# A hybrid layer in fp32r: low parts of 14 weight chunks by an accumulating DMA, the second input chunk in halves, score masks in pairs

## The chip, the cores and the metric

The kernel runs on one core of a Trainium2 chip. Its engines are TensorE (PE, with its weight loads PEld), VectorE (DVE), ScalarE (ACT), GpSimd (POOL) and SyncE (SP), which issues most DMAs. The metric is the device time of one execution in microseconds.

## What is computed

One layer: eight heads of block-sparse attention and four heads of an mLSTM share one input projection; their joined output goes through w_out, and a squared-ReLU MLP follows.

```python
D_MODEL = 1024; SEQ = 512; ATT_HEADS = 8; ATT_HEAD_DIM = 64; MLSTM_HEADS = 4; D_FF = 4096

def hybrid_layer(x, positions, ...):
    hdn = rms_norm(x, g_mix_pre)
    proj = hdn @ w_in
    aq, ak, av, mq, mk, mv, mo, mi, mf = jnp.split(proj, ...)
    q_a = partial_rope(to_heads(aq, ATT_HEADS), positions)
    k_a = partial_rope(to_heads(ak, ATT_HEADS), positions)
    att = moba_attention(q_a, k_a, v_a)
    ...
    hm = mlstm_chunkwise(q_m, k_m, v_m, ig, lf)
    ...
    mixed = jnp.concatenate([att, hm], axis=-1).astype(x.dtype)
    x = x + rms_norm(mixed @ w_out, g_mix_post)
    u = rms_norm(x, g_mlp_pre) @ w_up
    u = jnp.square(jax.nn.relu(u))
    return x + rms_norm(u @ w_down, g_mlp_post)
```

All inputs are float32. With 512 tokens and blocks of 256, attention is plain causal attention in effect: each of the four 128-query tiles of a head sees the keys up to its own end, and a triangular mask is added on the diagonal 128x128 block.

## The kernel before

Every float32 product is made of three fp32r matmuls: an operand is split into a high part (rounded to fp32r) and a low part (the rest), and high x high, high x low and low x high are summed in PSUM.

The weights come in chunks, numbered in the order of use: 0 to 3 for the mLSTM's q and k (mqk), 4 to 7 for the gates and part of v (gv, 392 columns a half), 8 to 11 and 16 to 19 for the attention's q and k (qk), 12 to 15 (vv) and 20 to 23 (av) for v, 24 to 27 for the output gate, 28 to 35 for w_out, from 36 on for the MLP. Each chunk is loaded by SP into one of three `raw` buffers (line 171). `split_to` (lines 180 to 200) then makes its parts in one of three `ws` buffers: ScalarE copies `raw` into `ws[:,0]`, which rounds it (line 197), and VectorE subtracts that from `raw` into `ws[:,1]` (line 198). For the odd chunks 5 to 35 GpSimd does the subtraction. `chunk(i)` asks for the split of chunk i+2 and the load of chunk i+4 when PE's program reaches chunk i. Within a slab PE takes, for each weight part, x-high by weight-high, then x-high by weight-low, then x-low by weight-high (in mqk: weight-high by x-high, weight-high by x-low, weight-low by x-high), so the low part is wanted a step or two after the high part.

At the start, x comes transposed in four chunks (`xr0` to `xr3`), with weight chunks 0 to 2 between them (lines 263 to 271). The first x chunk and weight chunk 0 are loaded in halves. `split_x` makes high and low parts of x (lines 252 and 253). After mqk, PE transposes a row of normalisation factors (`rstd_rows`, line 318 on; tiles rc, pb, rb), and gv follows.

PE's order is written by hand: `Flow` interleaves the side work (mLSTM and attention heads) with the weight slabs by planned times. The other engines are ordered by priorities, where a chunk's split ranks ahead (offset `BOOST`). In `att_head` each head handles its four score tiles in two pairs. For a tile it issues two fp32r matmuls (query by key-high, key-low), a third bf16 one that adds the mask (`identb` x `maskb`, line 672), then on VectorE the row maximum (line 674), on ScalarE the exponential (line 676), and on VectorE the reciprocal and the scaling by it (lines 677 and 678).

Of the kernel before, what the change touches and what calls it, by code (L numbers as in the profile page):

```python
# [15 lines left out]
F32 = mybir.dt.float32  # L16
# [4 lines left out]
OP = mybir.AluOpType  # L21
# [3 lines left out]
P = 128  # L25
S = 512
# [81 lines left out]
def kernel(  # L108
# [17 lines left out]
    nc = tc.nc  # L126
    f = lambda ap: ap.bitcast(F32)
# [3 lines left out]
    ring = ctx.enter_context(tc.tile_pool(name="ring", bufs=3))  # L131
# [3 lines left out]
    psa = ctx.enter_context(tc.tile_pool(name="psa", bufs=4, space=PSUM))  # L135
# [3 lines left out]
    specs = []  # L139
# [24 lines left out]
    raws, splits = {}, {}  # L164
    state = {"res": None, "load": 0, "split": 0}
# [8 lines left out]
    def load_to(i):  # L174
        while state["load"] <= min(i, len(specs) - 1):
            k = state["load"]
            raws[k] = load_raw(specs[k][0], specs[k][1], f"raw{k}")
            state["load"] += 1

    def split_to(i):  # L180
        while state["split"] <= min(i, len(specs) - 1):
            k = state["split"]
            if specs[k][2] == "res" and state["res"] is None:
                return
            load_to(k)
            _, n, where = specs[k]
            if where == "ring":
                ws = ring.tile([P, 2, 1024], F32R, tag="ws", name=f"ws{k}", bufs=3)
            else:
                ws = state["res"].tile([P, 2, 1024], F32R, tag="u", name=f"ws{k}")  # L190
            raw = raws.pop(k)
            parts = 2 if k == 0 else 1
            lo = nc.gpsimd if 3 < k < n_wo and k % 2 else nc.vector
            with tc.high_priority(offset=BOOST):
                for a in range(parts):
                    sl = slice(a * n // parts, (a + 1) * n // parts)
                    nc.scalar.copy(ws[:, 0, sl], raw[:, sl])  # L197
                    lo.tensor_tensor(ws[:, 1, sl], raw[:, sl], f(ws[:, 0, sl]), op=OP.subtract)  # L198
            splits[k] = ws
            state["split"] += 1  # L200

    def chunk(i):

        split_to(i + 2)
        load_to(i + 4)
        return splits[i]

    def mm(o, lh, rh, first, last, go_on=False):
        nc.tensor.matmul(o, lh, rh, start=first, stop=last, skip_group_check=go_on)  # L209
        flow.pe(max(o.shape[-1], 256) / 2.4 + 2.5)  # L210
# [6 lines left out]
    def tr(o, i, idn):  # L217
        nc.tensor.transpose(o, i, idn)  # L218
        flow.pe(109.0)
# [36 lines left out]
    xv = x_t.rearrange("p k n -> p (k n)")  # L256
    def spare(tag, name):
        return wk.tile([P, 1280], F32, tag=tag, name=name, **({"bufs": 3} if tag == "w5" else {}))

    xrs = [spare(("w5", "w5", "w5", "h5")[c], f"xr{c}") for c in range(4)]  # L260
    raws[0] = ring.tile([P, 1024], F32, tag="raw", name="raw0", bufs=3)
    state["load"] = 1
    for a in range(2):
        sl = slice(a * S, (a + 1) * S)
        nc.sync.dma_start(xrs[0][:, sl], xv[:, sl])
        nc.sync.dma_start(raws[0][:, sl], specs[0][0][:, sl])
    for c in range(1, 4):
        nc.sync.dma_start(xrs[c][:, 0:1024], xv[:, c * 1024:(c + 1) * 1024])
        if c < 3:
            load_to(c)  # L270
# [6 lines left out]
    for c in range(4):  # L277
        split_x(c, xrs[c])
        if c < 3:
            split_to(c)  # L280
# [140 lines left out]
    for c, ci in enumerate(slab_chunks["mqk"]):  # L421
        ws = chunk(ci)
# [9 lines left out]
    identb = one.tile([P, P], BF16, name="identb")  # L432
    maskb = one.tile([P, P], BF16, name="maskb")
# [216 lines left out]
    def att_head(g, h):  # L650
        e = h % 2
        half = slice(64 * e, 64 * e + 64)
        pr = 2 * g + h // 2
        hid = 4 * g + h
        prev = [f"st{g}a" if h < 2 else f"st{g}b"] + ([f"h{hid - 2}"] if hid >= 2 else [])
        for ii in ((0, 1), (2, 3)):
            yield dict(cond=prev if ii[0] == 0 else None, banks=2, hold=DLY["sh"])
            if ii[0] == 0:
                qs, ks, kls = stacks[g]
                if e == 0:  # L660
                    mix[pr] = kts.tile([P, 2, S], F32R, tag="kt", name=f"mix{pr}")
                    m32s[pr] = wk.tile([P, S], F32, tag="t32", name=f"m32_{pr}")
                pp = wk.tile([P, 1280], F32, tag="w5", name=f"pp{g}{h}", bufs=3)
                mxs = small.tile([P, NT], F32, tag="mxs", name="mxs", bufs=3)
                rs = small.tile([P, NT], F32, tag="rs", name="rs", bufs=3)
            for i in ii:
                n = (i + 1) * P
                sp = psa.tile([P, S], F32, tag="at", name=f"as{g}{h}{i}")
                iq = slice(i * P, (i + 1) * P)
                mm(sp[:, 0:n], qs[h][:, iq], ks[h][:, 0:n], True, False)  # L670
                mm(sp[:, 0:n], qs[h][:, iq], kls[h][:, 0:n], False, False)
                nc.tensor.matmul(sp[:, i * P:n], identb, maskb, start=False, stop=True)
                flow.pe(56)
                nc.vector.tensor_reduce(mxs[:, i:i + 1], sp[:, 0:n], axis=AX.X, op=OP.max, negate=True)  # L674
                po = pp[:, POFF[i]:POFF[i] + n]
                nc.scalar.activation(po, sp[:, 0:n], AF.Exp, bias=mxs[:, i:i + 1], accum_out=rs[:, i:i + 1])  # L676
                nc.vector.reciprocal(rs[:, i:i + 1], rs[:, i:i + 1])
                nc.vector.tensor_scalar(po, po, rs[:, i:i + 1], None, op0=OP.mult)
        ph = wk.tile([P, 1280], F32R, tag="h5", name=f"ph{g}{h}")
        pl = wk.tile([P, 1280], F32R, tag="l5", name=f"pl{g}{h}")  # L680
        for jj in ((0, 1), (2, 3)):
            yield dict(delay=DLY["pt"] if jj[0] == 0 else 0, banks=2, hold=DLY["pth"])
            for j in jj:
                n = S - j * P
                pt = psa.tile([P, S], F32, tag="at", name=f"pt{g}{h}{j}")
                for i in range(j, NT):
                    tr(pt[:, (i - j) * P:(i - j + 1) * P], pp[:, POFF[i] + j * P:POFF[i] + (j + 1) * P], ident)
                c = slice(OFF[j], OFF[j] + n)
                nc.scalar.copy(ph[:, c], pt[:, 0:n])
                nc.vector.tensor_tensor(pl[:, c], pt[:, 0:n], f(ph[:, c]), op=OP.subtract)  # L690
        yield dict(delay=DLY["ao"], banks=1, hold=1500, cond=f"av{g}")
        o = psa.tile([P, S], F32, tag="at", name=f"ao{g}{h}")
        for j in range(NT):
            c = slice(OFF[j], OFF[j] + S - j * P)
            mm(o[:, j * P:], av[g][j][:, h], ph[:, c], j == 0, False)
            mm(o[:, j * P:], av[g][j][:, h], pl[:, c], False, j == NT - 1)
        m32 = m32s[pr]
        nc.scalar.copy(m32[half], o[64:128])
        nc.vector.tensor_tensor(m32[half], o[0:64], m32[half], op=OP.add)
        if e == 1:  # L700
            nc.scalar.copy(mix[pr][:, 0], m32)
            nc.vector.tensor_tensor(mix[pr][:, 1], m32, f(mix[pr][:, 0]), op=OP.subtract)
        flow.flags.add(f"h{hid}")
# [5 lines left out]
    for g in range(2):  # L709
        flow.add(att_group(g))  # L710
        for h in range(4):
            flow.add(att_head(g, h))
# [42 lines left out]
    for i, c in enumerate(WO_ORDER):  # L755
        flow.until(need[c])
        ws = chunk(wo_chunks[0][i])
# [188 lines left out]
    at, bt = {}, {}  # L946
# [49 lines left out]
    for g in range(3):  # L996
        new_group(g + 1)
        for m in range(8):
            n = 7 * g + m
# [31 lines left out]
    for c in range(4):  # L1031
        ws = chunk(dn_chunks[0, c])
# [13 lines left out]
    for t in range(NT):  # L1046
        cuts = [(0, S)] if t < NT - 1 else [(0, 256), (256, 512)]
        yg = ygs[t]
        for a, b in cuts:
            pd = (psa if a == 0 else psm).tile([P, S], F32, tag="at" if a == 0 else "mm", name=f"dl{t}{a}")[:, a:b]  # L1050
            for m in range(8):
                c, kc = m // 2, slice((m % 2) * S + a, (m % 2) * S + b)
# [81 lines left out]
```

## Time and profile before

| | |
|---|---|
| median of 3 runs | 593.75 us (592.96 to 594.2) |
| profiled execution | 595.46 us, span 593.7 us, mean granted clock 0.995 |
| PE busy | 578.5 us (97%), 2895 matmuls |
| DVE busy | 429.4 us (72%) |
| ACT busy | 286.4 us (48%) |
| POOL busy | 72.6 us (12%) |
| DMA | 60.79 MB, mean 102 GB/s |
| chain that ended last | PE 87%, DVE 8%, ACT 2%, DMA 1% |

Busy time is the time in which an engine has an instruction in work; matmuls are pipelined, so a PE that is busy may still step more slowly than it can. The chain follows the last instruction back through whatever released each step. The granted clock is TensorE's, as a share of full speed.

### The profile page before, as it was taken

The page shows a single profiled execution, that of the slowest core. Times are in us where ns is not written, and L with a number is a line of the kernel's source. Part 1 is how long each engine was busy: PE and PEld are TensorE (multiplying, and loading weights), DVE is VectorE, ACT ScalarE, POOL GpSimd, SP SyncE. Part 2 cuts the span into 40 slices and gives each one's busy share as a digit, 9 for nine tenths or more (in the row PEclk, how much of TensorE's full clock was granted, in tenths as well). Part 3 has the DMA queues.
Part 4 walks back from the last instruction along what each step waited for, and adds up shares of the span by engine and source line. Part 5 has one row for each costly group of instructions (what it writes and reads, how often), then busy time and mean ns, then how long its engine had stood idle before and what let it go on. Part 6 is the DMA issues. An engine that isn't in the chain of part 4 may idle for free.

```text
span 593.7 us, 7757 instructions
## 1 busy us (share of the span) xinstructions
PE 578.5 (97%) x2895; PEld 488.6 (82%) x2895; DVE 429.4 (72%) x790; ACT 286.4 (48%) x505; POOL 72.6 (12%) x78
## 2 busy tenths in 40 slices
PE   8999999899999999999999999999999999999995
PEld 4898898688978888898888888888888888888884
DVE  5897868687996845865778685988667986856346
ACT  5664556467756654475344344344443443444211
POOL 0133341225311040000000000000000000000132
PEclk9999999899999999999999999999999999999999
DMA  7633121102311266007611363121543114013002
GB/s 281 258 135 115 63 71 55 35 20 72 107 71 36 73 230 231 0 1 257 257 54 36 110 218 132 36 68 40 198 156 106 36 36 142 35 36 129 14 35 108
DMA packets 18470, 60.79 MB, mean 102 GB/s; under 512 B 2432, under 2 KB 2432, under 8 KB 18432
## 3 DMA queue, kind: packets, MB, share of 16 engines
q1 hardware_dynamic: 18288, 60.28, 29.3%
q8 instruction: 23, 0.38, 0.3%
q14 instruction: 15, 0.12, 0.1%
q10 hardware_dynamic: 144, 0.01, 0.0%
HBM read 58.19 MB, written 2.10 MB: 102 GB/s over the span
## 4 chain that ended last, share of the span: by engine, by line
PE 87%; DVE 8%; ACT 2%; DMA 1%; issue 1%; SPq 0%; DVEq 0%; ACTq 0%
PE up L209 29%; PE pX L209 11%; PE qk L209 7%; PE pY L209 5%; PE mo L209 4%; PE dl L209 4%; PE ya L209 4%; PE dn L209 4%; PE gv L209 3%; PE pZ L209 3%; PE mqk L209 3%; PE vv L209 2%; PE yb L209 2%; PE ao L209 1%; PE as L209 1%; PE pt L218 1%
## 5 line engine op out<-in xcount | busy, mean ns | idle before, releaser
L209 PE MATMUL up<-hT,ws 128*128 128x512 f32 (+1 forms) x840 | 180.0, 372 | 0.4 <-DVE hT L811 0.4
L209 PEld LDWEIGHTS up<-hT,ws 128*128 128x128 f32 x840 | 148.3, 188 | 27.8 <-DVE hT L811 0.6
L197 ACT CAST ws<-raw 128x1024 fp32r<-128x1024 f32 (+3 forms) x77 | 76.3, 996 | 127.6 <-PE up L209 83.7
L198 DVE TENSOR_TENSOR ws<-raw,ws 128x1024 fp32r<-128x1024 f32 (+3 forms) x61 | 73.0, 1198 | 62.2 <-ACT ws L197 61.7
L904 ACT CAST w<-b 128x1024 fp32r<-128x1024 f32 x42 | 44.3, 1055 | 61.5 <-PE pX L209 27.2
L905 DVE TENSOR_TENSOR w<-b,w 128x1024 fp32r<-128x1024 f32 x42 | 51.4, 1223 | 25.9 <-ACT w L904 25.9
L209 PE MATMUL pX<-w,a 128*128 128x512 f32 x288 | 67.2, 389 | 0.0
L209 PEld LDWEIGHTS pX<-w,a 128*128 128x128 f32 x288 | 54.1, 188 | 11.2
L198 POOL TENSOR_TENSOR ws<-raw,ws 128x1024 fp32r<-128x1024 f32 (+3 forms) x16 | 36.5, 2284 | 115.2 <-ACT ws L197 79.9
L209 PE MATMUL qk<-ws,xT 128*128 128x512 f32 x192 | 49.2, 406 | 0.0
L1043 POOL TENSOR_TENSOR yg<-y,gp 128x512 f32<-128x512 f32 x4 | 5.2, 1299 | 337.4 <-DVE y L1038 337.2
L209 PEld LDWEIGHTS qk<-ws,xT 128*128 128x128 f32 x192 | 36.0, 193 | 7.0
L209 PE MATMUL pY<-w,a 128*128 128x512 f32 x144 | 33.6, 389 | 0.0
L209 PEld LDWEIGHTS pY<-w,a 128*128 128x128 f32 x144 | 27.0, 188 | 5.6
L876 DVE TENSOR_TENSOR b<-b,b 128x1024 f32<-128x1024 f32 x24 | 29.1, 1218 | 1.4 <-DMA b<-in_w_down_dram 1.3
L209 PE MATMUL mo<-ws,xT 128*128 128x512 f32 x96 | 25.9, 407 | 0.0
L209 PE MATMUL mqk<-xT,ws 128*128 128x512 f32 x96 | 23.5, 397 | 1.4 <-ACT ws L197 0.9
L209 PEld LDWEIGHTS mqk<-xT,ws 128*128 128x128 f32 x96 | 17.6, 188 | 7.4 <-ACT ws L197 2.2
L209 PE MATMUL yb<-ws,mix 128*128 128x512 f32 x96 | 23.1, 394 | 0.0
L209 PE MATMUL ya<-ws,mix 128*128 128x512 f32 x96 | 22.9, 394 | 0.0
L676 ACT ACTIVATE pp<-as,mxs 128x128 f32<-128x128 f32 (+3 forms) x32 | 16.8, 526 | 11.0 <-DVE mxs L674 10.9
L904 ACT CAST a<-u 128x1024 fp32r<-128x1024 f32 x17 | 17.8, 1050 | 8.8 <-DVE u L846 4.9
(283 smaller groups left out, 930.9 us busy)
## 6 DMA issues: line engine op xcount, KB each, us to landing
raw<-in_w_up_dram SPq DMA_DIRECT2D x32, 512.0 KB, 3.3
b<-in_w_down_dram SPq DMA_DIRECT2D x24, 512.0 KB, 4.4
raw<-in_w_in_dram SPq DMA_DIRECT2D x15, 512.0 KB, 3.3
raw<-in_w_out_dram SPq DMA_DIRECT2D x8, 512.0 KB, 3.3
raw<-in_w_down_dram SPq DMA_DIRECT2D x8, 512.0 KB, 3.2
xs<-in_x_dram SPq DMA_DIRECT2D x4, 512.0 KB, 8.7
x<-in_x_dram SPq DMA_DIRECT2D x4, 512.0 KB, 6.6
out_dram<-yg SPq DMA_DIRECT2D x8, 256.0 KB, 2.0
```

The source lines that it names most:

```text
L197: nc.scalar.copy(ws[:, 0, sl], raw[:, sl])
L198: lo.tensor_tensor(ws[:, 1, sl], raw[:, sl], f(ws[:, 0, sl]), op=OP.subtract)
L209: nc.tensor.matmul(o, lh, rh, start=first, stop=last, skip_group_check=go_on)
L218: nc.tensor.transpose(o, i, idn)
L676: nc.scalar.activation(po, sp[:, 0:n], AF.Exp, bias=mxs[:, i:i + 1], accum_out=rs[:, i:i + 1])
L876: nc.vector.tensor_tensor(o, a, b, op=op)
L904: nc.scalar.copy(o[:, 0], src)
L905: nc.vector.tensor_tensor(o[:, 1], src, f(o[:, 0]), op=OP.subtract)
L1043: nc.gpsimd.tensor_tensor(ygs[t][:, A], y[t][:, A], gp2[:, A], op=OP.mult)
```

## The change

Three edits. First, for the odd chunks from 5 to 31 (14 of the 16 that GpSimd split), ScalarE makes the low part's start: it writes the negative of `raw`, rounded, to `ws[:,1]`, and a DMA issued by GpSimd reads the chunk from DRAM once more and adds it there. Chunks 33 and 35 stay with GpSimd's subtraction. Second, the second x chunk and weight chunk 1 are loaded in halves, and chunk 1 is split in halves. Third, the scores of both tiles of a pair come first, then both masks in a row, then the work of VectorE and ScalarE on each.

```diff
-            parts = 2 if k == 0 else 1
+            parts = 2 if k < 2 else 1
...
                     nc.scalar.copy(ws[:, 0, sl], raw[:, sl])
-                    lo.tensor_tensor(ws[:, 1, sl], raw[:, sl], f(ws[:, 0, sl]), op=OP.subtract)
+                    if 3 < k < 32 and k % 2:
+
+                        nc.scalar.mul(ws[:, 1, sl], raw[:, sl], -1.0)
+                        nc.gpsimd.dma_start(ws[:, 1, sl], specs[k][0][:, sl], accum_op=OP.add)
+                    else:
+                        lo.tensor_tensor(ws[:, 1, sl], raw[:, sl], f(ws[:, 0, sl]), op=OP.subtract)
...
-    for c in range(1, 4):
+    raws[1] = ring.tile([P, 1024], F32, tag="raw", name="raw1", bufs=3)
+    state["load"] = 2
+    for a in range(2):
+        sl = slice(a * S, (a + 1) * S)
+        nc.sync.dma_start(xrs[1][:, sl], xv[:, 1024 + a * S:1024 + (a + 1) * S])
+        nc.sync.dma_start(raws[1][:, sl], specs[1][0][:, sl])
+    for c in range(2, 4):
...
+            sps = {}
             for i in ii:
                 n = (i + 1) * P
-                sp = psa.tile([P, S], F32, tag="at", name=f"as{g}{h}{i}")
+                sp = sps[i] = psa.tile([P, S], F32, tag="at", name=f"as{g}{h}{i}")
                 iq = slice(i * P, (i + 1) * P)
                 mm(sp[:, 0:n], qs[h][:, iq], ks[h][:, 0:n], True, False)
                 mm(sp[:, 0:n], qs[h][:, iq], kls[h][:, 0:n], False, False)
-                nc.tensor.matmul(sp[:, i * P:n], identb, maskb, start=False, stop=True)
+            for i in ii:
+                nc.tensor.matmul(sps[i][:, i * P:(i + 1) * P], identb, maskb, start=False, stop=True)
                 flow.pe(56)
+            for i in ii:
+                n = (i + 1) * P
+                sp = sps[i]
                 nc.vector.tensor_reduce(mxs[:, i:i + 1], sp[:, 0:n], axis=AX.X, op=OP.max, negate=True)
```

On GpSimd, at the gv slab, the two subtractions for chunks 5 and 7 (`ws5`, `ws7`) stood among the memsets that clear halves of the mLSTM's key tiles (`m2kl`, `m3kl`). Before:

```order
L198 TENSOR_TENSOR ws5_285<-raw5_230,ws5_285 128x784
L410 MEMSET m2kl0_344 64x512
L198 TENSOR_TENSOR ws7_412<-raw7_288,ws7_412 128x784
L410 MEMSET m2kl1_350 64x512
L410 MEMSET m3kl0_358 64x512
L410 MEMSET m3kl1_364 64x512
```

Now:

```order
L201 DMA ws5_289<-in_w_in_dram 128x784
L201 DMA ws7_417<-in_w_in_dram 128x784
L421 MEMSET m2kl0_349 64x512
L421 MEMSET m2kl1_355 64x512
L421 MEMSET m3kl0_363 64x512
L421 MEMSET m3kl1_369 64x512
```

The two transfers stand in a row, and all four memsets behind both.

On ScalarE, at the same place, between the casts of chunks 4 to 7 and the first parts of the mLSTM's queries (`m0q`, `m1q`). Before:

```order
L197 CAST ws4_256<-raw4_201 128x784
L197 CAST ws5_285<-raw5_230 128x784
L197 CAST ws6_383<-raw6_259 128x784
L398 ACTIVATE m0q0_327<-t32_0_325 64x512
L398 ACTIVATE m0q1_330<-t32_0_325 64x512
L398 ACTIVATE m1q0_335<-t32_1_333 64x512
L398 ACTIVATE m1q1_338<-t32_1_333 64x512
L197 CAST ws7_412<-raw7_288 128x784
```

Now:

```order
L197 CAST ws4_260<-raw4_205 128x784
L197 CAST ws5_289<-raw5_234 128x784
L200 ACTIVATE ws5_289<-raw5_234 128x784
L197 CAST ws6_388<-raw6_263 128x784
L409 ACTIVATE m0q0_332<-t32_0_330 64x512
L409 ACTIVATE m0q1_335<-t32_0_330 64x512
L197 CAST ws7_417<-raw7_293 128x784
L200 ACTIVATE ws7_417<-raw7_293 128x784
```

Line 200 is the multiplication by -1; it follows its chunk's cast, and chunk 7's two passes now stand ahead of the two `m1q` parts.

On PE, the second pair of score tiles of one head (`as`), up to the next head group's transposes (`tp`). Before:

```order
L209 MATMUL as_1719<-a03k_1134,a01q_1091 128x384
L209 MATMUL as_1719<-a03kl_1135,a01q_1091 128x384
L672 LDWEIGHTS identb
L672 MATMUL as_1719<-maskb,identb 128x128
L209 MATMUL as_1727<-a03k_1134,a01q_1091 128x512
L209 MATMUL as_1727<-a03kl_1135,a01q_1091 128x512
L672 LDWEIGHTS identb
L672 MATMUL as_1727<-maskb,identb 128x128
L218 MATMUL tp_1737<-cs,qk_1508 128x128
```

Now:

```order
L214 MATMUL as_1733<-a03k_1145,a01q_1101 128x384
L214 MATMUL as_1733<-a03kl_1146,a01q_1101 128x384
L214 MATMUL as_1736<-a03k_1145,a01q_1101 128x512
L214 MATMUL as_1736<-a03kl_1146,a01q_1101 128x512
L685 LDWEIGHTS identb
L685 MATMUL as_1733<-maskb,identb 128x128
L685 LDWEIGHTS identb
L685 MATMUL as_1736<-maskb,identb 128x128
L223 MATMUL tp_1751<-cs,qk_1521 128x128
```

The first tile's mask has moved behind the second tile's two steps.

## Rows read from the trace of the kernel before

**Rows 1.** The page: busy time, share of the span and instructions of each engine, and the chain that ended last, by engine.

```profile
PE 578.5 (97%) x2895; PEld 488.6 (82%) x2895; DVE 429.4 (72%) x790; ACT 286.4 (48%) x505; POOL 72.6 (12%) x78
PE 87%; DVE 8%; ACT 2%; DMA 1%; issue 1%; SPq 0%; DVEq 0%; ACTq 0%
```

**Rows 2.** Busy time by stage: the stretch and its length in us, then the busy time and instructions of PE, PEld, DVE, ACT and POOL, the granted clock, the DMA engines' share and GB/s.

```profile
5.09:13.51 8.42, 7.31 (x26) 4.55 (x26) 4.85 (x8) 4.77 (x7) 0.00 (x0) 1.00 0.95 352
...
29.90:47.20 17.30, 17.30 (x100) 17.30 (x99) 15.10 (x25) 10.71 (x18) 7.53 (x7) 1.00 0.42 144
...
74.00:109.00 35.00, 31.42 (x194) 29.53 (x192) 28.09 (x70) 20.96 (x49) 9.63 (x13) 1.00 0.20 61
```

**Rows 3.** Timeline of PE at the start: start us, length us, what ran, and in brackets the idle time before it and what ended that.

```profile
8.64 3.28 PE L209 MATMUL mqk<-xT,ws 128*128 128x512 f32 x12 [0.22 <-ACT ws L197]
12.26 0.73 PE L209 MATMUL mqk<-xT,ws 128*128 128x512 f32 x2 [0.33 <-ACT ws L197]
13.51 16.21 PE L209 MATMUL mqk<-xT,ws 128*128 128x512 f32 x70 [0.52 <-DVE ws L198]
```

**Rows 4.** The chain, in order of time, at the end of the mqk slab and through gv: start us, length us, what.

```profile
29.72 0.44 PE pb L218 x4
30.16 17.08 PE gv L209 x96
```

**Rows 5.** Timeline of ScalarE and VectorE around the second x chunk and weight chunk 1.

```profile
9.86 1.34 ACT L252 ACTIVATE xT<-xr,gcol 128x512 fp32r<-128x512 f32 x2 [1.27 <-DMA xr<-in_x_t_dram]
...
11.15 1.05 ACT L197 CAST ws<-raw 128x1024 fp32r<-128x1024 f32 x1
12.23 1.22 DVE L198 TENSOR_TENSOR ws<-raw,ws 128x1024 fp32r<-128x1024 f32 x1 [0.20 <-ACT ws L197]
```

**Rows 6.** Timeline of ScalarE, VectorE and GpSimd around the start of gv. In order: the casts of chunks 4 and 5, the copy for the transposes, GpSimd's low part of chunk 5, VectorE's of chunk 4, the copy after the transposes, VectorE's low part of chunk 6, the cast of chunk 7, GpSimd's low part of chunk 9.

```profile
26.30 1.58 ACT L197 CAST ws<-raw 128x784 fp32r<-128x784 f32 x2
...
27.91 0.42 DVE L323 COPY rc<-rstd 128x512 f32<-128x512 f32 x1
27.96 2.99 POOL L198 TENSOR_TENSOR ws<-raw,ws 128x784 fp32r<-128x784 f32 x1 [9.54 <-ACT ws L197]
28.24 0.97 DVE L198 TENSOR_TENSOR ws<-raw,ws 128x784 fp32r<-128x784 f32 x1
...
30.20 0.69 DVE L326 COPY rb<-pb 128x512 f32<-128x512 f32 x1 [0.99 <-PE pb L218]
30.80 0.98 DVE L198 TENSOR_TENSOR ws<-raw,ws 128x784 fp32r<-128x784 f32 x1
...
35.04 0.85 ACT L197 CAST ws<-raw 128x784 fp32r<-128x784 f32 x1
...
44.24 2.40 POOL L198 TENSOR_TENSOR ws<-raw,ws 128x1024 fp32r<-128x1024 f32 x1 [4.55 <-issue]
```

**Rows 7.** DMA issues, with the KB of each and the median us from issue to landing. The first row is of the loads issued from 16 to 21 us, the other two are of 28.9 to 31.9 us, where the first is a queue's row: packets, MB and the share of 16 engines.

```profile
raw<-in_w_in_dram SPq DMA_DIRECT2D x3, 392.0 KB, 8.5
...
q1 hardware_dynamic: 144, 0.40, 38.7%
...
raw<-in_w_in_dram SPq DMA_DIRECT2D x1, 392.0 KB, 2.8
```

**Rows 8.** Groups of instructions by form over the whole span: busy us, mean ns of one, and the idle time before them with what ended it. ScalarE's casts of weight chunks, then GpSimd's low parts.

```profile
L197 ACT CAST ws<-raw 128x1024 fp32r<-128x1024 f32 x63 | 65.9, 1052 | 113.9 <-PE up L209 83.7 <-issue 17.5 <-DMA raw<-in_w_out_dram 5.3
...
L197 ACT CAST ws<-raw 128x512 fp32r<-128x512 f32 x6 | 3.7, 617 | 3.8 <-DMA raw<-in_w_in_dram 3.2 <-POOL qk L622 0.6
...
L197 ACT CAST ws<-raw 128x784 fp32r<-128x784 f32 x4 | 3.3, 842 | 1.9 <-issue 1.9
...
L198 POOL TENSOR_TENSOR ws<-raw,ws 128x1024 fp32r<-128x1024 f32 x10 | 25.2, 2522 | 84.3 <-ACT ws L197 49.0 <-issue 23.5 <-DVE pp L678 11.8
```

**Rows 9.** Timeline of PE at one pair of score tiles: the first tile's second step, its mask, and the second tile's two steps. Lengths overlap, since matmuls are pipelined; the starts tell the pace.

```profile
124.48 0.33 PE L209 MATMUL as<-a02kl,a00q 128*128 128x384 f32 x1
124.66 0.23 PE L672 MATMUL as<-maskb,identb 128*128 128x128 bf16 x1
124.70 0.47 PE L209 MATMUL as<-a02k,a00q 128*128 128x512 f32 x1
125.01 0.40 PE L209 MATMUL as<-a02kl,a00q 128*128 128x512 f32 x1
```

**Rows 10.** Timeline rows of GpSimd, VectorE and PE: GpSimd's low part of chunk 23 and a scaling of scores beside it, PE's wait at 156.40 and its first step with chunk 23, and a scaling of the same form at another place.

```profile
147.68 1.28 POOL L198 TENSOR_TENSOR ws<-raw,ws 128x512 fp32r<-128x512 f32 x1 [4.27 <-ACT ws L197]
147.75 1.29 DVE L678 TENSOR_SCALAR pp<-pp,rs 128x128 f32<-128x128 f32 x1
...
156.40 0.30 PE L218 MATMUL pt<-cs,pp 128*128 128x128 f32 x1 [0.82 <-DVE a12kl L412]
156.46 0.72 PE L209 MATMUL av<-ws,xT 128*128 128x256 f32 x4
...
170.22 0.28 DVE L678 TENSOR_SCALAR pp<-pp,rs 128x128 f32<-128x128 f32 x1
```

**Rows 11.** PE's wait in the attention part and the slab's steps behind it, from the timeline, and one microsecond of the table by stretches (columns as in rows 2).

```profile
108.69 0.33 PE L209 MATMUL sp<-m1q,m3k 128*128 128x128 f32 x1 [2.57 <-DVE dd L569]
...
108.97 4.50 PE L209 MATMUL qk<-ws,xT 128*128 128x512 f32 x12
...
110.00:111.00 1.00, 1.00 (x4) 0.81 (x3) 0.90 (x2) 1.00 (x2) 0.00 (x0) 0.50 0.00 0
```

## What was predicted before the change was run

> **What bounds the kernel now.** I read the page's busy line and the chain that ended last first [rows 1]. TensorE is busy 578.5 of 593.7 us and carries 87% of the chain; VectorE comes next with 8%. So a saving counts only where PE waits or takes a step longer than it must. The table by stage [rows 2] says where that can be. The chunks from 32 on, which the change leaves alone, fill more than the second half of the span. In what comes before, PE stands idle in few places: 1.1 us of the 8.42 around the second chunk at the start and 3.6 us of the 35 from 74 to 109. PE also steps at half clock for some 3 us after 109. The timelines, read at these places, show what is late. At the start [rows 3] PE waits 0.33 us for ScalarE's cast of the second chunk and 0.52 us for VectorE's low part of it, and runs without a gap from 13.51 to 29.72, where the chain goes on to the transposes and the gv slab [rows 4]. Behind both waits stands a transfer: the second x chunk has landed only when ScalarE takes it up at 9.86, the chunk's weights at 11.15 [rows 5], with the DMA engines 95% busy [rows 2]. In the attention part PE waits 2.57 us at 108.69 for VectorE, which is busy 28.09 of the 35 us before [rows 2], and behind that wait the clock is granted at 0.50, the lower of its two levels (1.2 GHz) [rows 11].
>
> **The start by halves: -0.8.** Two loads of 512 KB become four of half the size, in the order x, weights, x, weights, and the two passes of the second chunk's split become four. The bytes are the same, so the last half lands where the whole did, near 11.1; the first half of x and of the weights land before that, I reckon by 9.9, where the whole x chunk landed. A cast of 512 columns is 0.62 us [rows 8], so the first half's high part is there by about 10.5 to 11.2 and its low part some 0.7 us later (half of the 1.22 us that the whole took, and a little [rows 5]). PE ends the first chunk at 11.92 [rows 3] and then needs only that first half; the second half is wanted twelve steps of 0.23 us later (70 of them take 16.21 us [rows 3]), at 14.7, long after 12.5. Both waits go, 0.33 + 0.52 = 0.85. What is late next is the end of the slab: it comes at 28.9 instead of 29.72. The four transposes there need VectorE's copy that ends at 28.33, and the next slab needs VectorE's low part of chunk 4, which ends at 29.21 [rows 6]; the slab's second step would now stand at 29.3. That is tight, so I take -0.8, with -0.3 (that low part or the copies slip) and -0.9 as ends.
>
> **The masks in a row: -0.8.** The rows at 124.48 [rows 9] show the price of one: the score step of 384 columns before it takes 0.18 us, as a gv step of 392 does [rows 4], the mask itself holds PE for 0.04 (124.66 to 124.70), but the fp32r step behind it takes 0.31 (124.70 to 125.01), where one of 512 columns otherwise takes 0.23. A mask thus makes the next step 0.08 us longer. With two in a row, one of each pair has a mask behind it, not an fp32r step. The trace has no mask behind a mask. If it takes the 0.04 us of a mask, 16 pairs give 16 x 0.08 = -1.3; if the cost merely moves to it, nothing. I take -0.05 a pair, -0.8. The first tile's maximum can start only after the second tile's two steps, some 0.55 us later. VectorE has other work for that time, and in the attention part the waits of PE that I price are for other products (108.69 and 156.40).
>
> **GpSimd's subtractions gone: -0.4.** Fourteen of its sixteen low parts, 2.5 us each for 1024 columns [rows 8], leave the engine. It was 12% busy, so its own time is worth nothing. But VectorE stood still beside one: a 128x128 multiplication that takes 0.28 us elsewhere took 1.29 beside GpSimd's 1.28 at 147.7 [rows 10]. Work of VectorE alone leads from there to PE's wait of 0.82 us at 156.40. Without those 1.01 us the wait could go whole, unless other work then moves in front; half of it is -0.4, the ends are 0 and -0.8.
>
> **Fourteen more passes on ScalarE: +0.3.** The multiplication by -1 reads and writes what the cast does; at its rows [rows 8] that is 8 x 1.052 + 4 x 0.842 (768 and 784 columns) + 2 x 0.617 = 13.0 us. ScalarE is 48% busy, which covers most of it. Where it isn't covered is 74 to 109 us, three such passes: ScalarE's casts and copies there feed the VectorE that PE waits for. A pass of 0.84 that delays that chain fully costs 0.8 each and may lengthen the stretch at half clock. A third of one is +0.3; the ends are +1.5 (two in full) and -1.0, since VectorE loses GpSimd's company there too.
>
> **Fourteen accumulating transfers: +0.7.** Each reads the chunk from HBM again and adds it to the negated high part, 6.2 MB in all; the DMA engines' share is 0.42 and 0.20 in two of these stages [rows 2], so bandwidth is there. What counts is when each lands. For chunk 5 ScalarE's two casts end at 27.88 [rows 6], its negation at 28.72, so GpSimd issues at about 28.8. Before, GpSimd had this low part at 30.95, and the first step of chunk 5 stood at 30.0 + 24 x 0.178 = 34.3 (the gv slab: 96 steps in 17.08 [rows 4]); with the earlier start it is 33.5, and the second step, the first to read the low part, 33.7. That leaves 4.9 us. The trace has no accumulating and no GpSimd-issued transfer. A plain one of this size took 2.8 us with free queues and 8.5 in the crowd at the start [rows 7]; these are my bounds. Reading its target as well as its source, it should be nearer to two of the quiet ones: 5.6, so 34.4, and PE waits 0.7. The ends are 0 (up to 4.9) and +3.6 (8.5). The other chunks have more. Chunk 7 is negated by 36.7 (its cast ends at 35.89 [rows 6]) and wanted at 30.0 + 72 x 0.178 + 0.2 = 43.0, 6.3 us; chunk 9 by 45.2 (GpSimd began at 44.24 [rows 6] as the cast ended) and wanted one slab end and 24 steps on, 47.24 (30.16 + 17.08) + 24 x 0.23 + 0.2 = 53.0, 7.8 us; chunk 23, cast by 147.7 as GpSimd began, by 148.3 and wanted behind its first step at 156.46 [rows 10], 156.6, 8.3 us. GpSimd's queue now holds four memsets behind the transfer of chunk 7, where one stood ahead of it and three behind; they start when ScalarE has negated chunk 7, near 36.7, earlier than the three behind GpSimd's subtraction of chunk 7 could, which began only as the cast ended.
>
> "DMA: Bandwidth & Descriptors" of the Trainium skill, in "Anatomy of one DMA", fits a GpSimd-issued transfer as about 2.0 us plus its bytes at 436 GB/s, an estimate of 2.9 us for 392 KB. That is the quiet row's 2.8; it has nothing on the added read. By it alone this term would be 0 and the sum 592.0.
>
> **The sum.** -0.8 - 0.8 - 0.4 + 0.3 + 0.7 = -1.0 us. The profiled execution took 595.46 with a span of 593.7; it would become 594.5 and 592.7. It lies 1.7 above the median of the timed runs, 593.75, to which I apply the same difference: **592.75**.
>
> **The rivals.**
> 1. *The stretch before 109 is relieved.* VectorE, free of GpSimd, reaches the product for which PE waits 2.57 us [rows 11] earlier, and PE doesn't fall to half clock: twelve steps at 108.97 took 4.50, 1.7 more than 12 x 0.23. Half of the wait and half of that loss are 1.3 + 0.9 = 2.2 us below the sum: 590.55. For it: VectorE nearly never pauses there. Against: I saw its stretching only beside GpSimd at 147.7, not there.
> 2. *The accumulating transfers land late* (slower than before). If one takes 9 us, chunk 5 is late by 4.1 instead of 0.7, and with PE later chunks 7 and 9 are then covered; chunk 23 adds 0.6. Net 3.4 + 0.6 = +4.0: 596.75. It comes out slower than before from a first transfer of 6.6 us (1.0 more late), and beyond what can be told from 7.8. For it: the same size took 8.5 here in a crowd. Against: at 28.8 the queues are nearly empty (38.7% busy from 28.9 to 31.9 [rows 7]).
> 3. *GpSimd can't issue beside VectorE.* In [rows 10] the two engines shut each other out. If an issue needs a pause of VectorE, and chunk 5's misses the one before the copy at 30.20, it goes out at about 31.8, when VectorE's next low part has ended [rows 6], and lands at 37.4: late by 3.7, a total near 595.75. For it: VectorE is busy 15.10 of the 17.30 us after 29.90 [rows 2]. Against: it does pause, 0.99 us before 30.20, and most of its work there are other forms than that of [rows 10].
> 4. *ScalarE's passes delay the stretch before 109* by one to two whole passes of 0.84 in place of a third of one, and the half clock lasts as much longer, for up to 0.8: 593.3 to 594.9.
>
> "SBUF - State Buffer" of the Trainium skill, in "SBUF: two separate sides", has rival 3 as a rule: transfers issued by GpSimd have their descriptors written by it, and it is locked out while VectorE holds the port that they share. The row at 147.7 agrees on the lock between the two engines' instructions; no row here shows an issue.
>
> **How the numbers follow.** The forecast, 592.0 to 594.0, has 0.47; rival 1 has 0.17, rival 2 0.13, rival 3 0.08, rival 4 0.15. About 0.2% of the time, 1.2 us, is what a measurement of this kernel can tell from no change, so faster means below 592.55 and slower above 594.95. Faster holds rival 1 and somewhat less than half of the forecast, 0.38; slower holds rivals 2 and 3 and a little of 4, 0.23; the rest, 0.39, is no change that can be told. The range leaves out the far ends of rivals 1 and 2: 590.4 to 597.0.
>
> **What would show it.** Start: no wait of PE between 11.9 and 28.9 and the gv slab beginning 0.8 us earlier; wrong, if a wait for VectorE's low part of chunk 1 or 4 appears. Masks: the step behind the second mask 0.31, the second mask itself within 0.1 us of the first. Transfers: on GpSimd's queue, the median from issue to landing for 392 KB and 512 KB (5.6 and 7 us by my estimate), and a PE wait for a DMA at the second step of chunk 5 of 0.7 us, none elsewhere. GpSimd: no VectorE multiplication of 1.29 us at 147. ScalarE: the wait at 108.69 as long as now, and the half clock too. The forecast is wrong most likely through the transfers, if PE waits for one later than chunk 5, or through the stretch before 109.

## The result and the profile after

The kernel became slower. Ten runs of the changed kernel have a median of 598.11 us (595.51 to 601.34), ten of the kernel before 594.33 (592.96 to 596.05); the ratio is 1.0053, with a 95% interval of 1.0035 to 1.0071, some +3.2 us (the two medians lie 3.8 apart). The prediction was 592.75 in a range of 590.4 to 597.0, with 0.23 for slower: the sign was wrong, and the time lies beyond the range.

The profiled execution is the fastest of the ten, with a span of 593.7 us, the same as that of the profile before; the other nine have spans of 594.4 to 599.6. So I read in this trace what the change does where nothing more is lost, and in a second one, of 599.1, what is added in a longer execution.

The page of the changed kernel, busy time and chain, against [rows 1]:

```profile
PE 576.9 (97%) x2895; PEld 488.2 (82%) x2895; DVE 424.3 (71%) x791; ACT 296.7 (50%) x520; POOL 52.9 (9%) x78
PE 85%; DVE 9%; ACT 2%; DMA 2%; issue 1%; DVEq 0%; SPq 0%; ACTq 0%
```

ScalarE is busy 10.3 us more: the 14 passes add up to 13.1 (13.0 were reckoned), part of it in overlap with other instructions. GpSimd is busy 20 less. The chain now has 2% of DMA.

Its table by stage, columns as in [rows 2]:

```profile
5.09:13.51 8.42, 8.30 (x36) 6.50 (x36) 5.26 (x9) 4.98 (x9) 0.00 (x0) 1.00 0.96 342
...
29.90:47.20 17.30, 15.84 (x89) 15.52 (x88) 12.90 (x23) 10.67 (x17) 3.82 (x6) 1.00 0.71 197
...
74.00:109.00 35.00, 31.63 (x193) 29.78 (x191) 28.11 (x70) 23.14 (x51) 7.63 (x13) 1.00 0.36 87
```

PE's idle time has moved from the first stretch (1.1 us before, 0.1 now) to the gv slab (none before, 1.5 now), and the stretch before 109 is as it was. The timeline of PE shows both, against [rows 3]:

```profile
5.35 22.37 PE L214 MATMUL mqk<-xT,ws 128*128 128x512 f32 x96
27.83 0.66 PE L223 MATMUL pb<-cs,rc 128*128 128x128 f32 x4
28.24 5.03 PE L214 MATMUL gv<-ws,xT 128*128 128x392 f32 x25
34.73 10.59 PE L214 MATMUL gv<-ws,xT 128*128 128x392 f32 x58 [1.46 <-DMA ws<-in_w_in_dram]
```

All 96 steps of mqk run in one piece. PE starts gv 1.7 us earlier than before (28.24 against 29.91), makes the 24 steps of chunk 4 and the first of chunk 5, and waits 1.46 us for the transfer. The chain says how long that took, from GpSimd's issue at 28.18:

```profile
27.09 0.77 ACT ws L200
27.86 0.31 issue
28.18 6.50 DMA ws<-in_w_in_dram
34.68 0.04 issue
34.73 12.90 PE gv L214 x71
```

And the DMA view, the new queue alone: first its packets, MB and the share of 16 engines that the packets took, then its issues:

```profile
q0 software_dynamic: 2016, 6.31, 6.2%
...
ws<-in_w_in_dram POOLq DMA_DIRECT2D x6, 512.0 KB, 7.5
...
ws<-in_w_in_dram POOLq DMA_DIRECT2D x2, 392.0 KB, 6.7
```

A second trace of the same kernel (the first run below), of an execution of 599.1 us: PE at gv, and four stretches of the table by time.

```profile
35.47 12.86 PE L214 MATMUL gv<-ws,xT 128*128 128x392 f32 x62 [2.45 <-DMA ws<-in_w_in_dram]
```

```profile
36.00:37.00 1.00, 1.00 (x4) 1.00 (x4) 0.96 (x2) 0.95 (x2) 0.89 (x3) 0.50 1.02 410
37.00:38.00 1.00, 1.00 (x4) 1.00 (x4) 0.99 (x3) 0.62 (x1) 0.92 (x2) 0.50 0.80 200
...
112.00:113.00 1.00, 1.00 (x4) 0.81 (x4) 0.68 (x3) 0.94 (x2) 0.37 (x1) 0.50 0.00 0
...
115.00:116.00 1.00, 1.00 (x4) 0.81 (x3) 0.43 (x1) 1.00 (x2) 0.00 (x0) 0.50 0.00 0
```

Here the same transfer takes 7.2 us, the wait is 2.45, and behind it the clock is granted at 0.50, 1.2 GHz, from 35.7 to 39.1: the 71 steps behind the wait take 14.46 us, against 12.90 in the first trace. Behind PE's wait at 109, which is 2.5 or 2.6 us in every trace of this study, the half clock lasts 6.8 us here, 3.4 in the trace before and not at all in the first trace after; the twelve steps there take 5.43 us against 4.50 [rows 11] and 2.95. Both traces have all 2895 matmuls in the same order, so their starts can be compared one by one: PE is 0.2 us earlier at gv, 0.7 later behind the wait (1.0 of longer wait), 2.3 later a dozen steps on (1.5 of half clock), 5.1 later once the half clock after 109 is over (2.9), and 0.3 more is lost at 226, where PE's weight load waits 0.4 for the transfer of chunk 31. That makes the 5.4.

The other executions have no trace, but each has its mean granted clock. Of the sixteen of the changed kernel (ten here, six below) eight have 0.988 to 0.990; of the 29 of the kernel before on the chip of the second trace none is below 0.994, and of 93 on other chips one is as low as 0.990. Span times granted clock tells what an execution would take at full clock, the rest is lost to half clock. By that the changed kernel takes 592.2 us (median, in both sets) against 590.3 before, and loses 4.4 and 5.5 us (means) against 2.8. So some 1.8 us of the loss is there at full clock, and the half clock adds 1.6 to 2.7 on average.

### The profile page after: what moved, and what is told of

It is laid out like the page before. It is cut to its first block, busy times and chain, and to the rows that moved or that the text cites. A ratio compares the mean times of both kernels' runs of the same rounds, so it can differ in the third digit from the quotient of the medians.

```text
span 593.7 us, 7809 instructions
## 1 busy us (share of the span) xinstructions
PE 576.9 (97%) x2895; PEld 488.2 (82%) x2895; DVE 424.3 (71%) x791; ACT 296.7 (50%) x520; POOL 52.9 (9%) x78
## 3 DMA queue, kind: packets, MB, share of 16 engines
q1 hardware_dynamic: 18576, 60.28, 29.8%
## 4 chain that ended last, share of the span: by engine, by line
PE 85%; DVE 9%; ACT 2%; DMA 2%; issue 1%; DVEq 0%; SPq 0%; ACTq 0%
PE up L214 29%; PE pX L214 11%; PE qk L214 7%; PE pY L214 5%; PE dl L214 4%; PE dn L214 4%; PE mqk L214 4%; PE ya L214 3%; PE mo L214 3%; PE pZ L214 3%; PE gv L214 2%; PE vv L214 2%; PE yb L214 2%; PE ao L214 1%; PE as L214 1%
## 5 line engine op out<-in xcount | busy, mean ns | idle before, releaser
L203 DVE TENSOR_TENSOR ws<-raw,ws 128x1024 fp32r<-128x1024 f32 (+3 forms) x62 | 71.8, 1159 | 60.1 <-ACT ws L197 59.8
L214 PE MATMUL qk<-ws,xT 128*128 128x512 f32 x192 | 47.8, 397 | 0.0
L862 DVE TENSOR_TENSOR u<-u 128x512 f32<-128x512 f32 x32 | 21.9, 684 | 0.0
```

Of the source, the lines that this page charges most:

```text
L862: nc.vector.tensor_tensor(d, d, d, op=OP.mult)
```

## The experiments

Ratios are to the kernel before on the same chip, with their 95% intervals; 0.001 is 0.6 us.

**The changed kernel again** (no edit).

> The changed kernel once more, for its spread and a second trace. Theory A (PE's wait for the accumulating transfer of chunk 5, and half clock behind it): the median is 596 to 599 against some 594.3 before, a slower execution has a wait of over 1.46 us at the gv slab, followed by a stretch granted 0.50. Theory B (the later order of ScalarE and VectorE in the attention part): the same time, but the half clock stands behind 70 us, at a wait in the attention part, and the wait at gv stays at 1.5.

Measured: 1.0067 (1.0042 to 1.0092), median 599.46, and the trace above. Both places of theory A and B have half clock; what differs from the first trace begins at gv, as A has it, and the longest part of it, 2.9 of 5.4 us, stands after 109.

**Two edits without the transfers.**

```diff
-                    if 3 < k < 32 and k % 2:
-                        nc.scalar.mul(ws[:, 1, sl], raw[:, sl], -1.0)
-                        nc.gpsimd.dma_start(ws[:, 1, sl], specs[k][0][:, sl], accum_op=OP.add)
-                    else:
-                        lo.tensor_tensor(...)
+                    lo.tensor_tensor(...)
```

> Halves and masks alone, all low parts where they were before. Theories A and B: without the transfers and the extra passes both costs go, and the start's gain and the masks' (1.9 and 0.2 in the trace of the changed kernel) stay: 1.5 to 3 us below before, some 592. Theory C (halves or masks cost): within 0.5 us of the changed kernel, 597.

Measured: 1.0012 (0.9997 to 1.0027). All theories missed: the transfers with ScalarE's passes are most of the loss, 0.4 to 0.55 points, but the halves and masks do not gain either. Its trace has PE waits of 0.85 at 199.7 us for `pl` (the low part of a head's transposed scores) and of 1.10 at 154.6 for `a12kl` (the low part of a head's keys), which come back below.

**The transfers alone** (the first hunk of the diff on the kernel before).

> The accumulating transfers alone, with the start and the masks of before. Theory A: the gv slab begins 1.7 us later, so the transfer of chunk 5 is nearly there when it is wanted (a wait of 0 to 0.5 us), and the time is near that of before, 594 to 595.5. Theory B: slower by the passes, 597 to 599.

Measured: 1.0030 (1.0016 to 1.0045), and in its trace a wait of 1.77 us at gv:

```profile
36.34 10.94 PE L214 MATMUL gv<-ws,xT 128*128 128x392 f32 x60 [1.77 <-DMA ws<-in_w_in_dram]
```

PE wants chunk 5 later without the halves, but GpSimd issues later too (29.15 against 28.18), and the transfer takes 7.15 us: A's "nearly there" was wrong, its place right. At full clock this kernel takes 592.3 us (median), as the changed one does, and it loses no more to half clock than the kernel before (3.0 against 2.8): the wait alone did not bring the extra half clock. Behind that wait the trace goes as that of before, but for PE's wait at 156, which is 0.57 instead of 0.82, and for the half clock after 109, which it doesn't have.

**Chunk 5 back on GpSimd.**

```diff
-                    if 3 < k < 32 and k % 2:
+                    if 5 < k < 32 and k % 2:
```

> The changed kernel with chunk 5's low part back on GpSimd; the other 13 transfers stay. Theory A: the wait at gv is gone, 592 to 593.5, under before. Theory B: no better than the changed kernel less 1.5 us, 595 to 597.

Measured: 1.0016 (1.0005 to 1.0027), median 595.92: most of the loss is gone, not all. The transfer of chunk 7 is now the one that PE waits for:

```profile
28.26 13.24 PE L214 MATMUL gv<-ws,xT 128*128 128x392 f32 x73
42.55 4.36 PE L214 MATMUL gv<-ws,xT 128*128 128x392 f32 x23 [1.05 <-DMA ws<-in_w_in_dram]
```

Without chunk 5's wait ahead of it, PE wants chunk 7 at 41.5, and it was issued at 35.94 and took 6.6. A wait that was removed has moved to the next chunk.

**The halves alone** (the second edit), **the masks alone** (the third).

> The halves at the start alone. If the start's gain lasts (PE 1.5 to 2 us earlier at the gv slab, nothing given back): 1.5 us below before, ratio 0.997. If the spread of the kernel with halves and masks comes from the start (transfers landing at other times in each execution), the ratio is near 1.000 and the spread over 2 us.

> The masks in a row alone. In the trace of the changed kernel each pair gained some 0.05, and 1.0 us was lost at 201 us, where chunk 30's cast now stands ahead of a copy of transposed scores on ScalarE. If this edit moved that cast: the same wait of PE for VectorE's pl at 201, a ratio of 1.000 to 1.001. If ScalarE's extra passes moved it: no such wait, ratio 0.999.

Measured: halves 0.9989 (0.9975 to 1.0003), masks 1.0012 (1.0000 to 1.0024). The trace of the halves has a wait that is in neither other trace, PE's for `gts`, the gates read out of gv's accumulators:

```profile
46.59 3.71 PE L209 MATMUL qk<-ws,xT 128*128 128x512 f32 x15 [1.35 <-DVE gts L461]
```

```profile
42.24 2.40 POOL L198 TENSOR_TENSOR ws<-raw,ws 128x1024 fp32r<-128x1024 f32 x1 [3.76 <-issue]
42.29 2.62 DVE L419 CAST m3k<-m3k 64x512 fp32r<-64x512 f32 x1
```

GpSimd began chunk 9's low part 0.05 us ahead of VectorE's copy of `m3k` (keys of the mLSTM), and that took 2.62 us in place of 0.42, as in [rows 10]; the evacuation of gv's accumulators comes late by it. In the trace before, the copy came first, ahead of GpSimd at 44.24:

```profile
43.50 0.42 DVE L413 CAST m3k<-m3k 64x512 fp32r<-64x512 f32 x1
```

The halves do not always bring this about: in the two traces of halves and masks without transfers the copy began 0.37 and 0.75 ahead of GpSimd and took 0.42.

The masks alone shorten the pairs (below), but PE waits for pl at the last head:

```profile
198.74 1.05 ACT L197 CAST ws<-raw 128x1024 fp32r<-128x1024 f32 x1
...
199.70 0.47 ACT L694 CAST ph<-pt 128x384 fp32r<-128x384 f32 x1
199.83 1.22 DVE L198 TENSOR_TENSOR ws<-raw,ws 128x1024 fp32r<-128x1024 f32 x1 [0.29 <-ACT ws L197]
...
201.67 0.52 PE L218 MATMUL pt<-cs,pp 128*128 128x128 f32 x3 [0.85 <-DVE pl L695]
```

Chunk 30's cast and low part stand between the first and the second part of the transposed scores on both engines, so VectorE frees the accumulator 1 us later. The changed kernel's trace has the same wait (0.99 at 200.60). PE's wait for a12kl at 156 is longer as well, 1.11 in place of 0.82; it is 1.09 to 1.11 in all three traces with the masks and with chunk 23's split as before, and 0.83 in the two with the halves and without the masks. No run here tells what moves it.

**The transfers from chunk 9 on, alone** (`8 < k`).

> The accumulating transfers alone, for the odd chunks 9 to 31; chunks 5 and 7 stay with GpSimd. If only the first transfers are late (wanted 5 to 7 us after their issue): no PE wait for a transfer, and the time of before or 0.3 below it, ratio 0.999 to 1.000. If ScalarE's passes cost by themselves: ratio 1.001 to 1.002, with waits for ScalarE or VectorE between 80 and 180 us.

Measured: 1.0007 (0.9992 to 1.0023), a PE wait of 0.30 for chunk 9 at 53.42 and no other for a transfer. Against the transfers alone (1.0030) the loss goes with the early two, though the two intervals overlap a little; the others cost nothing that is clear of noise, and gain nothing.

**Halves and masks, chunk 30 at ordinary priority.**

```diff
-            with tc.high_priority(offset=BOOST):
+            with tc.high_priority(offset=BOOST if k != 30 else 0):
```

> Halves and masks with chunk 30's split at ordinary priority, which puts its cast behind the copies of that head on ScalarE. If the cast's place costs the 1.0 us at 201: that wait is gone and the ratio is 0.0017 below that of halves and masks, 0.9995. If not: the same ratio of 1.001.

Measured: 0.9989 (0.9974 to 1.0005), and no wait for pl near 201. The ratio is 0.0023 below that of halves and masks, as expected if that cast's place is the loss of the masks, though the two intervals overlap. (In its trace the first twelve steps of mqk are slow, and gv begins 0.3 us later than before, so it does not show the start's gain.)

**ScalarE's passes without the transfers.**

```diff
-                        nc.gpsimd.dma_start(ws[:, 1, sl], specs[k][0][:, sl], accum_op=OP.add)
+                        nc.gpsimd.tensor_tensor(ws[:, 1, sl], raw[:, sl], f(ws[:, 1, sl]), op=OP.add)
```

> The changed kernel with its 14 extra passes on ScalarE, but GpSimd adds raw to the negated high part (a tensor_tensor as before the change) in place of the transfers. If the passes cost by themselves: ratio 1.003 or more, waits of PE for ScalarE's pp near 148 and 173 us as in the changed kernel (0.4 and 0.2). If it is the transfers: the ratio of halves and masks, 1.001, and no wait at gv above 0.3 us.

Measured: 1.0015 (0.9999 to 1.0031), against 1.0012 for halves and masks. The waits at 148 and 173 are there (0.4 and 0.2), yet the difference is only 0.2 us, less than the intervals can tell.

**The transfers without the addition.**

```diff
-                        nc.gpsimd.dma_start(ws[:, 1, sl], specs[k][0][:, sl], accum_op=OP.add)
+                        nc.gpsimd.dma_start(ws[:, 1, sl], specs[k][0][:, sl])
```

> The changed kernel with the 14 GpSimd transfers writing the chunk in place of adding it (the low parts then are the weights themselves, so the products are wrong by that; the order of all work is the same). If the addition makes the transfer slow: 392 KB lands in about 3 us, PE's wait at gv is gone, and the ratio is 1.002. If the way through GpSimd does: still 6 to 6.7 us, a wait of 1.5 at gv, ratio 1.005.

Measured: 0.9990 (0.9976 to 1.0004). That is below what either theory had. The program order, ScalarE's passes and the bytes read from HBM are those of the changed kernel; the addition is gone, and with it 0.3 us of each issue on GpSimd. The transfer takes 4.4 us, and PE has no wait in gv:

```profile
q0 software_dynamic: 2016, 6.31, 3.1%
...
ws<-in_w_in_dram POOLq DMA_DIRECT2D x6, 512.0 KB, 4.7
...
ws<-in_w_in_dram POOLq DMA_DIRECT2D x2, 392.0 KB, 4.4
```

```profile
28.41 17.33 PE L214 MATMUL gv<-ws,xT 128*128 128x392 f32 x96
```

This is the run that settles the sign: with 2.3 to 2.8 us less per transfer, +0.53% (+0.67% the second time) becomes -0.10%. Of its twelve executions none has a span over 594.3, where the changed kernel goes to 599.6 and more, and its loss to half clock is that of the kernel before (3.2 and 3.1). The same packets and bytes took the DMA engines half the time without the addition, 3.1% against 6.2%; SP's plain loads take 29.5% for 60.28 MB, the same per MB as the GpSimd transfers without the addition.

**The transfer for chunk 23 alone, with halves, masks and chunk 30 as above** (`k == 23`); **all of the change with transfers from chunk 9 on, and chunk 30 as above**.

> Halves, masks and chunk 30 at ordinary priority, with the transfer for chunk 23 alone, where GpSimd's subtraction held VectorE up for 1.0 us. If the hold counts: PE's wait of 1.1 at 156 us falls to 0.2, and the ratio is 0.997 to 0.998. If ScalarE's pass for chunk 23 takes it back at 148 us: 0.9985 to 0.9995, as without it.

> The changed kernel with transfers from chunk 9 on only (5 and 7 stay with GpSimd) and chunk 30 at ordinary priority. If the early transfers and chunk 30's cast are the whole loss: no wait at gv above 0.3 us, none for pl at 201, ratio 0.997 to 0.999. If the passes cost too: 1.000 to 1.002.

Measured: 0.9982 (0.9965 to 1.0000) and 0.9989 (0.9971 to 1.0007). In the first, PE's wait at 156 is 0.2 as expected, and a wait of 0.4 for ScalarE's `pp` (the exponentials of the scores) at 148 has come, as the other theory had it; the interval doesn't tell it from 0.9989. Its trace has the copy of m3k at 2.59 us again, and the wait of 1.35 for gts behind it. The second has neither the wait at gv nor that near 201; the loss of the changed kernel is gone with the two early transfers and chunk 30's place.

**Halves with the transfer for chunk 9 alone; halves, masks and chunk 30 with those for 9 and 23.**

> Halves, with the transfer for chunk 9 alone. If GpSimd's low part of chunk 9 holds VectorE's copy of m3k near 42 us (2.6 us in place of 0.42) and so takes back the start's gain in part of the executions: no such copy, no PE wait for gts at 47, ratio 0.996 to 0.998 against 0.9989 for halves alone, unless the transfer itself comes late (wanted 8 us after its issue, so at most 0.3). If the start's gain is lost elsewhere: 0.9985 to 1.000 again.

> Halves, masks, chunk 30 at ordinary priority, and the transfers for chunks 9 and 23 alone, where GpSimd's subtraction was seen to hold VectorE. If the two holds are what GpSimd's low parts cost: ratio 0.995 to 0.997. If not: that of chunk 23 alone, 0.998.

Measured: 0.9974 (0.9959 to 0.9989) and 0.9968 (0.9946 to 0.9989). Without GpSimd's low part of chunk 9 the halves gain 0.26% instead of 0.11%, though the two intervals overlap: the copy of m3k takes 0.42, and PE passes from gv to qk without a wait. The last one, with two of the fourteen transfers, has the lowest ratio, some 1.9 us below the kernel before; its interval overlaps that of the same kernel without any transfer (0.9989). In its trace no wait for a transfer, for gts or for pl is left:

```profile
PE sp L214 <- DVE dd L580: 2.6, 1, 2.6
...
PE tp L223 <- DVE dd L568: 0.6, 1, 0.6
```

## Why the prediction was wrong

The term that turned the sign is the transfers: the run without the addition is no slower than the kernel before. The masks failed by a step of their own, and the gain forecast for GpSimd's subtractions was taken back.

**The start, -0.8 forecast.** Right in mechanism, and larger in the trace. Step by step against the trace before, PE gains 0.49 at 12.26 and 0.69 at 13.51, 1.2 us in the trace of every kernel with the halves; the steps right behind a wait are slow as well, which I had not counted beside the 0.85 of waits. Not all of the earlier start of gv is theirs: some 0.8 us is gained at the first chunk's second half (8.64 before, a wait of 0.22 and slow steps), which the trace of the masks alone doesn't have either. What I left out is that GpSimd's and VectorE's work then meet at another moment: in the trace of the halves alone 1.35 of the gain was given back at the end of gv.

**The masks, -0.8 forecast, +0.7 alone (1.0012).** The pairs are nearly as reasoned. One in the changed kernel:

```profile
123.31 0.33 PE L214 MATMUL as<-a02kl,a00q 128*128 128x384 f32 x1
123.47 0.40 PE L214 MATMUL as<-a02k,a00q 128*128 128x512 f32 x1
...
123.94 0.28 PE L685 MATMUL as<-maskb,identb 128*128 128x128 bf16 x2
124.04 1.63 PE L214 MATMUL qk<-ws,xT 128*128 128x512 f32 x6
```

From the first step of 384 columns to the step behind the masks this pair takes 0.91 us (123.13 to 124.04) against 0.98 before (124.31 to 125.29), so 0.07 is gained where 0.05 was forecast. The first pair of each head, of 128 and 256 columns, gains only 0.01 to 0.02 (0.56 against 0.58 at the first one); over all 16 pairs that is some 0.7 in the trace of the masks alone. The step that failed is "the first tile's maximum can start only after the second tile's two steps [...] VectorE has other work for that time": with the maxima and exponentials shifted, the order on ScalarE and VectorE changed, and chunk 30's split then stood ahead of what PE waits for near 201 us, 0.85 to 1.0; the wait at 156 grew by 0.3. I had compared the order of PE, GpSimd and ScalarE at the start, and not that of ScalarE at the end of the attention part.

**GpSimd's subtractions, -0.4 forecast.** PE's wait at 156 went from 0.82 to 0.20 in the changed kernel, but one of 0.42 for ScalarE came at 148, behind the new pass of chunk 23. That leaves 0.2. I had found one of the two holds seen in the traces; the other, at chunk 9, isn't in the trace before, where the two engines missed each other by 0.3 us.

**ScalarE's passes, +0.3 forecast.** About +0.2 by the run that has them without the transfers, with intervals of 1 us either way; the waits behind them are 0.4 at 148 and 0.2 at 172, not before 109. Rival 4 did not come. Rival 1 came in the first trace (no half clock after 109), but without its cause, as the wait there is as long as ever, and not in the second.

**The transfers, +0.7 forecast.** The place was right, the size not. The issue came at 28.18 (28.8 reckoned), the step that wants the low part at 33.3 (33.7), and the transfer took 6.50 us where 5.6 was the estimate: 1.46 of wait. In the second trace it is 7.2, and 2.45. "Nearer to two of the quiet ones" was right for the addition, which doubles the time on the DMA engines (6.2% against 3.1%), but it began from too low a base: a GpSimd transfer without the addition takes 4.4, against 2.8 for a plain load by SP. How much of that is the way through GpSimd and how much the loads beside it is open: SP's load of 512 KB issued in the same two microseconds took 6.5, and 4.9 in the run without the addition, so the crowd there is in part the addition's own. Nor is a crowd needed: the transfer of 512 KB at 55.49, with one load beside it, took 7.5.

The second failure is as large: I priced the wait by its own length. In the second trace PE's clock falls behind it, which costs 1.5 us for a wait of 2.45, and the half clock after 109 is longer in the same execution; the mean clocks show more half clock in half of the executions, worth 1.6 to 2.7 us on average. That this comes of the wait alone is not shown: the transfers alone have a wait of 1.77 and no more half clock than before.

In the list of rivals the second, the late transfer, is what happened, with its threshold: at 6.6 us of transfer it said "slower than before", and it was 6.5 and 7.2; a total beyond its 596.75 came by the clock, which was not in it. It got 0.13 because I read its chance from the queues at 28.9 to 31.9 in the trace before, where the new transfers weren't. Rival 3 has no support: GpSimd's issue took 1.0 us at 28.18, with VectorE at work throughout, and the transfers without addition landed in time.

The sum of the three edits measured one by one is -0.11 + 0.12 + 0.30 = +0.31%, that of all together +0.53 and +0.67. That the halves bring PE to chunk 5 sooner and so turn into wait there fits this, but the intervals are too wide to show it. With the transfers' +0.7 taken out, the forecast's sum is -1.7 us; the run without the addition measured -0.6 (-1.4 to +0.2), so the other terms came out some 1 us short of the forecast; the masks (-0.8 forecast, +0.7 by their own run) are enough to explain it.

**What stays open.** Why the half clock after 109 lasts 0, 3.4 or 6.8 us behind the same wait of 2.5 us: of the sixteen traces seven have none, eight have 3.4 and one has 6.8, and the two of the changed kernel have 0 and 6.8. At which places the executions with a low mean clock lost it is not known, as only two of the changed kernel have a trace.

## What to carry to other kernels

Work moved from an engine to a transfer must be checked by when its result is wanted, chunk by chunk: the two earliest of the fourteen lost what the start had won, and the lowest ratio came with only the two that stood where GpSimd and VectorE were seen to hold each other up. Where the trace shows half clock behind waits, give a PE wait a range that goes beyond its length. And when an edit shifts a dependence on PE, compare the static order of the other engines to the end of the part, not just at the edit.

## What had not been expected of the hardware

An accumulating transfer into SBUF took 6.5 to 7.2 us for 392 KB and 5.5 to 8.5 (median 7.5) for 512 KB in the two traces of the changed kernel; the same transfer without the addition had medians of 4.4 and 4.7, and a plain load by SP took 2.8 (392 KB, the quiet row) and 3.3 (512 KB, median). With the addition the packets took the DMA engines twice the time. Whether GpSimd holds VectorE up went by which of them came first: a copy took 2.62 us when GpSimd was 0.05 ahead of it, and 0.42 when the copy was first, so small shifts elsewhere can switch the hold on or off.
